# Distance between the two operands' addresses in products of 256 columns

## The chip, the cores and the metric

One core of a Trainium2 chip runs the whole kernel. The metric is device time in microseconds of one execution; the time of a kernel is the median of its runs.

## The reference

One block of an encoder for a sequence of 1024 tokens with 1024 channels, all in float32. The input is normalised and multiplied by one wide matrix, which feeds three mixers side by side: dilated sliding-window attention, grouped-query attention with normalised and rotated queries and keys, and cross-attention to 256 memory rows. Each has a gate, is projected, and the three are merged, projected once more, normalised and added to the input. Cut to what bears on this change:

```python
h = rms_norm(x, g_pre[layer])
a_qkv, bq, bk, bv, mq, ga, gb, gm, mg = jnp.split(h @ w_in[layer], split_at, axis=-1)
...
qb_ = axial_rope(rms_norm(bq.reshape(b, s, B_HEADS, HEAD_DIM), q_norm[layer]), row_pos, col_pos)
kb_ = axial_rope(rms_norm(bk.reshape(b, s, B_KV_HEADS, HEAD_DIM), k_norm[layer]), row_pos, col_pos)
...
kvm = rms_norm(mem, g_mem[layer]) @ w_mem_kv[layer]
km, vm = ...   # 4 heads of 128, 256 memory rows
sm = jnp.einsum('bshd,bnhd->bhsn', mq.reshape(b, s, M_HEADS, M_HEAD_DIM), km)
pm = jax.nn.softmax(sm * (M_HEAD_DIM ** -0.5), axis=-1)
om = jnp.einsum('bhsn,bnhd->bshd', pm, vm)
```

## The kernel before, in words

Every float32 matrix is split into a high part, rounded to the type that TensorE multiplies in one pass, and a low part, the rest. A product of two matrices is then three products: high by high, low by high, high by low. `hh[k]` and `hl[k]` (k = 0 to 7) are the high and low part of the normalised input, 128 channels by 1024 tokens each; `wh` and `wl` those of a tile of weights.

A product has two operands in on-chip memory: the one that is loaded into the array first (128 columns here; the profile calls it LDWEIGHTS) and the moving one, which is streamed through it (256 or 512 columns). In this text "weights" is the loaded operand, whatever it holds. In `PE.matmul(dst, a, b)` the weights are `a`, the moving operand is `b`.

The first stages, in the order in which they run:

1. `kv_proj` (line 354): keys and values of the grouped-query attention for all tokens. Eight tiles of channels, eight of tokens, three products each: 192 products, weights `hh` or `hl`, moving `wbh` or `wbl` with 256 columns. The operands of tile k are made by ScalarE (`hh`, line 255) and VectorE (`hl`, line 256) while the products of the tile before run. Behind the first half of its last tile stand eight transposes (line 242).
2. Two gate units (lines 128, 130, 132): products of 512 columns, beside which the norms of the keys run on VectorE, ScalarE and GpSimd.
3. `add_kv` (line 526): keys and values of the memory, eight units of 24 products; weights `wh` or `wl`, moving `mh` or `ml`, 256 columns.
4. Query units, woven together: `proj_tok` (lines 284, 286, 288) has 384 products, weights `hh` or `hl`, moving `wbh` or `wbl`, 256 columns. `m_att`, the memory attention, uses `passes` (line 110) for its scores (weights `mqh`, `mql`, moving `kmh`, `kml`) and its values (weights `vmh`, `vml`, moving `mph`, `mpl`), 192 products of 256 columns. Between them stand units of 512 columns (lines 128 to 132) and transposes (lines 590 and 700).

```python
for k in range(8):                                                   # proj_tok
    PE.matmul(dst, hh[k][:, t], th[:, k], start=k == 0, stop=False)
    PE.matmul(dst, hl[k][:, t], th[:, k], start=False, stop=False)
    PE.matmul(dst, hh[k][:, t], tl[:, k], start=False, stop=k == 7)
...
passes(sv[:, j], [(qh[:, t], kmh[:, h]), (qh[:, t], kml[:, h]), (ql[:, t], kmh[:, h])])   # scores
terms += [(vmh[:, kt, h], ph[:, kt]), (vmh[:, kt, h], pl[:, kt]), (vml[:, kt, h], ph[:, kt])]
passes(o[:, 0:256], terms)                                           # values
```

The order on TensorE is written out by the program (`weave` takes turns between two generators by costs in nanoseconds that are written in the code); addresses play no part in it. Behind these stages come the grouped-query attention (lines 775 to 809), the value projection (line 1314, products of 512 columns alone) and the rest.

Tiles come from pools, which hand out addresses in the order of the calls. The pool `st` (input tiles `xk`, later `mh` and `ml` in their places, tables) and, when it has closed, `qn` and `mt` (tiles of the memory attention) grow from the left; `kvl`, `ml` and `mb` (`wbh`, `wbl`, tables of the queries) lie at the right end, each placed against its right neighbour, so that a longer `mb` begins further left. A pad is a tile that nothing uses: it only moves what stands behind it (or, in a pool at the right, what stands ahead of it). A tile of weights of 128 columns is 512 bytes long in each partition, and all slices of 128 columns of one tile have one address modulo 512. In the kernel before, the address of the moving operand and that of the weights are equal modulo 512 in every product of 256 or 512 columns but the 128 of line 809 (the attention's values, 64 columns of weights) and the 6 of line 1977.

Of the kernel before, what the change touches and what calls it, by code (L numbers as in the profile page):

```python
# [8 lines left out]
F32 = mybir.dt.float32  # L9
# [8 lines left out]
P = 128  # L18
# [15 lines left out]
def block(ctx: ExitStack, tc: tile.TileContext, x, xT, memT, cst, msk, bcst, tabA, gpost,  # L34
# [28 lines left out]
    def pss1():  # L63
        return bank["p"].tile([P, 512], F32, name="s1", tag="s1", bufs=bank["n"][1])

    def pst():
        bank["i"] += 1
        return bank["p"].tile([P, 4, 128], F32, name="tr", tag="t", bufs=bank["n"][2])

    def pso():  # L70
        return bank["p"].tile([P, 512], F32, name="ov", tag="o", bufs=bank["n"][3])
# [17 lines left out]
    def split(dst_h, dst_l, src):  # L89
        A.activation(dst_h, src, AF.Copy)  # L90
        V.tensor_tensor(dst_l, src, dst_h.bitcast(F32), op=OP.subtract)  # L91
# [15 lines left out]
    def passes(out_ps, terms):  # L107
        n = len(terms)
        for i, (a, b) in enumerate(terms):
            PE.matmul(out_ps, a, b, start=i == 0, stop=i == n - 1)  # L110
# [107 lines left out]
    def pool(name, side="left"):  # L218
        p = tc.tile_pool(name=name, bufs=1, side=side, reuse_waits="tile")
        return p, p.__enter__()  # L220
# [4 lines left out]
    startp, st = pool("start")  # L225
    kvp, kvl = pool("kvl", "right")
    mlp, ml = pool("ml", "right")
    mbp, mb = pool("mb", "right")
# [4 lines left out]
    vmh = ml.tile([P, 2, 4, 128], R, name="vmh")  # L233
    vml = ml.tile([P, 2, 4, 128], R, name="vml")

    xk = [st.tile([P, S], F32, name=f"xk{k}") for k in range(8)]
    acc = st.tile([P, S], F32, name="acc")

# [27 lines left out]
    def fetch_wb(c0):  # L266
        raws = []
        for i in range(2):
            raw = wp.tile([P, 1024], F32, name="wr", bufs=WR)
            raws.append(raw.rearrange("p (k f) -> p k f", k=4))  # L270
        return raws, mb.tile([P, 8, 256], R, name="wbh"), mb.tile([P, 8, 256], R, name="wbl")
# [162 lines left out]

    PROJ = 8 * 24 * 109.0
    raws, *wkv = fetch_wb(512)
    mb.tile([P, 112], F32, name="pad")

    def load_wkv(i):
        nc.sync.dma_start(raws[i // 2][:, i % 2 * 2:i % 2 * 2 + 2], wb[:, 2 * i:2 * i + 2, 512:768])  # L440
# [113 lines left out]
    QN = [ql_.tile([P, 8, 64], F32, name=f"qn{T}") for T in range(NT)]  # L554
    mtp, mt_ = pool("mt")
    fp["p"] = mt_

    def m_att(h):
        qh, ql = MQ[h]
        if h == 0:  # L560
            mt_.tile([P, 48], F32, name="pad")
        for _ in range(4):
            yield 250
        st = {}

        def scores(n):
            sv = pss1().rearrange("p (t k) -> p t k", t=2)
            nm = mt_.tile([P, 2], F32, name="mnm", bufs=3)
            l = mt_.tile([P, 2], F32, name="mls", bufs=3)
            pm = mt_.tile([P, 2, 256], F32, name="pm", bufs=2)  # L570
            for j in range(2):
                t = slice((2 * n + j) * 128, (2 * n + j) * 128 + 128)
                passes(sv[:, j], [(qh[:, t], kmh[:, h]), (qh[:, t], kml[:, h]), (ql[:, t], kmh[:, h])])
            V.tensor_reduce(nm, sv, axis=AX.X, op=OP.min)
            V.tensor_tensor(nm, nm, rcol[:, 2 * n:2 * n + 2], op=OP.mult)
            for j in range(2):
                A.activation(pm[:, j], sv[:, j], AF.Exp, scale=nrcol[:, 2 * n + j:2 * n + j + 1], bias=nm[:, j:j + 1],
                             accum_out=l[:, j:j + 1])
            rl = mt_.tile([P, 2], F32, name="mrl", bufs=4)
            V.reciprocal(rl, l)  # L580
            for j in range(2):
                fp["mv"] = V.tensor_scalar(pm[:, j], pm[:, j], rl[:, j:j + 1], None, op0=OP.mult)
            st[n] = pm

        def trans(n):
            pm = st[n]
            tp = pst().rearrange("p (k t) q -> p k t q", k=2)
            for kt in range(2):
                for j in range(2):
                    PE.transpose(tp[:, kt, j, :], pm[:, j, kt * 128:kt * 128 + 128], ident)  # L590
            ph = mt_.tile([P, 2, 256], R, name="mph", bufs=2)
            pl = mt_.tile([P, 2, 256], R, name="mpl", bufs=2)
            split(ph, pl, tp.rearrange("p k t q -> p k (t q)"))
            st[n] = (ph, pl)

        def pv(n):
            ph, pl = st.pop(n)
            o = pso()
            terms = []
            for kt in range(2):  # L600
                terms += [(vmh[:, kt, h], ph[:, kt]), (vmh[:, kt, h], pl[:, kt]), (vml[:, kt, h], ph[:, kt])]
            passes(o[:, 0:256], terms)
            om = mt_.tile([P, 256], F32, name="om", bufs=2)
            A.activation(om, o[:, 0:256], AF.Copy)
            nc.sync.dma_start(od[2, h, :, n * 256:n * 256 + 256], om)

        for n in range(7):
            if n < 4:
                scores(n)
            yield 654  # L610
            if 0 <= n - 2 < 4:
                trans(n - 2)
            yield 436
            if 0 <= n - 3 < 4:
                pv(n - 3)
            yield 654
# [46 lines left out]
    early[len(queue)] = lambda: load_w(wu[U_G + 11])  # L663
    weave(1)
    weave(2, m_att(0), M_COST, 1.2)
    weave(2, m_att(1), M_COST, 1.2)
    weave(1, m_att(2), M_COST, 1.0)
    weave(1, m_att(3), M_COST, 1.0)
    while pend:
# [1692 lines left out]
```

## Time and profile before

| what | value |
|---|---|
| median of 3 runs | 1372.11 us (1370.52 to 1373.05) |
| the profiled execution's own time | 1370.94 us |
| its span, first to last instruction | 1369.1 us |
| TensorE clock granted, mean | 0.998 |
| TensorE busy | 1349.7 us, 99% of the span |
| VectorE, ScalarE, GpSimd busy | 74%, 48%, 42% |
| products on TensorE | 8303 records |

The durations that the profile gives for a product hold its way through the array and overlap with those of its neighbours (a product of 256 columns is shown as some 283 ns). How long a product takes in a stream is the distance from one start to the next; it is read from the chain of work, where rows of equal products are merged with their count, or from the starts in the timeline.

### The profile page before, as it was taken

The page shows a single profiled execution, that of the slowest core. Times are in us where ns is not written, and L with a number is a line of the kernel's source. Part 1 is how long each engine was busy: PE and PEld are TensorE (multiplying, and loading weights), DVE is VectorE, ACT ScalarE, POOL GpSimd, SP SyncE. Part 2 cuts the span into 40 slices and gives each one's busy share as a digit, 9 for nine tenths or more (in the row PEclk, how much of TensorE's full clock was granted, in tenths as well). Part 3 has the DMA queues.
Part 4 walks back from the last instruction along what each step waited for, and adds up shares of the span by engine and source line. Part 5 has one row for each costly group of instructions (what it writes and reads, how often), then busy time and mean ns, then how long its engine had stood idle before and what let it go on. Part 6 is the DMA issues. An engine that isn't in the chain of part 4 may idle for free.

```text
span 1369.1 us, 22888 instructions
## 1 busy us (share of the span) xinstructions
PE 1349.7 (99%) x8303; PEld 1091.0 (80%) x8303; DVE 1018.1 (74%) x1836; ACT 655.5 (48%) x1388; POOL 579.8 (42%) x443
## 2 busy tenths in 40 slices
PE   8999999999999999999999999999999999999997
PEld 7899987666666788988888888888888777778886
DVE  7868667777777398767777786687877666768977
ACT  7544456656654445333333333333335676763332
POOL 0516702666577200244465554555552134663003
PEclk9999999999999999999999999999999999999999
DMA  6356522222244569524333333322347778986455
GB/s 252 108 170 215 186 109 101 100 74 98 74 126 147 203 219 286 163 70 127 112 108 124 108 123 116 114 94 92 110 127 256 234 213 239 271 233 227 148 189 185
DMA packets 125489, 213.81 MB, mean 156 GB/s; under 512 B 32480, under 2 KB 64576, under 8 KB 125376
## 3 DMA queue, kind: packets, MB, share of 16 engines
q1 hardware_dynamic: 116064, 198.42, 45.2%
q10 hardware_dynamic: 9312, 13.93, 2.8%
q8 instruction: 65, 1.06, 0.3%
q14 instruction: 48, 0.39, 0.1%
HBM read 145.92 MB, written 66.38 MB: 155 GB/s over the span
## 4 chain that ended last, share of the span: by engine, by line
PE 92%; DVE 2%; POOL 2%; ACT 1%; issue 1%; DMA 1%; SPq 0%; DVEq 0%; POOLq 0%; ACTq 0%
PE s L1314 35%; PE d L1903 6%; PE s L1224 4%; PE s L2127 4%; PE ov L809 3%; PE sc L2045 3%; PE d L130 3%; PE d L128 3%; PE d L132 3%; PE s L1275 3%; PE s L1587 2%; PE tr L775 2%; PE s L794 2%; PE s L793 2%; PE d L526 2%; PE d L2127 2%
## 5 line engine op out<-in xcount | busy, mean ns | idle before, releaser
L800 POOL TENSOR_TENSOR bl<-bl,bp 128x512 f32<-128x512 f32 x96 | 133.0, 1385 | 54.1 <-ACT bp L796 48.6
L1314 PE MATMUL s<-hh,vS 128*128 128x512 f32 x400 | 131.1, 389 | 0.0
L1314 PE MATMUL s<-vA,vS 128*128 128x512 f32 x450 | 106.1, 389 | 0.0
L91 DVE TENSOR_TENSOR vS<-vot,vS 128x512 fp32r<-128x512 f32 x75 | 89.4, 1192 | 19.9 <-ACT vS L90 19.9
L1314 PEld LDWEIGHTS s<-vA,vS 128*128 128x128 f32 x450 | 84.5, 188 | 17.5
L796 ACT ACTIVATE bp<-s 128x512 f32<-128x512 f32 x128 | 75.6, 595 | 43.9 <-PE s L794 42.9
L776 DVE TENSOR_REDUCE bn<-tr 128x1 f32<-128x512 f32 x128 | 85.0, 684 | 13.7 <-PE tr L775 12.6
L132 PE MATMUL d<-hh,wl 128*128 128x512 f32 x224 | 89.4, 399 | 0.0
L128 PE MATMUL d<-hh,wh 128*128 128x512 f32 x224 | 89.2, 398 | 0.0
L130 PE MATMUL d<-hl,wh 128*128 128x512 f32 x224 | 89.1, 398 | 0.0
L1314 PEld LDWEIGHTS s<-hh,vS 128*128 128x128 f32 x400 | 75.1, 188 | 15.6
L1599 ACT ACTIVATE pra<-pra,sts 128x192 f32<-128x192 f32 (+1 forms) x176 | 72.4, 415 | 12.5 <-DVE sts L1598 12.1
L1314 PE MATMUL s<-hh,wl 128*128 128x512 f32 x200 | 78.1, 391 | 0.0
L1314 PE MATMUL s<-hl,wh 128*128 128x512 f32 x200 | 77.9, 389 | 0.0
L1314 PE MATMUL s<-hh,wh 128*128 128x512 f32 x200 | 77.8, 389 | 0.0
L1314 PE MATMUL s<-hl,vS 128*128 128x512 f32 x200 | 77.8, 389 | 0.0
L1598 DVE CUSTOM_DVE_ANT_0 pra<-s,mask 128x192 f32<-128x192 f32 (+1 forms) x192 | 48.9, 309 | 33.3 <-PE s L1587 18.7
L1058 POOL TENSOR_TENSOR vot<-wr 128x512 f32<-128x512 f32 x13 | 22.2, 1706 | 111.4 <-DVE wl L91 111.4
L1318 ACT ACTIVATE vv<-s 128x512 f32<-128x512 f32 x50 | 29.9, 598 | 82.4 <-PE s L1314 48.5
L809 PE MATMUL ov<-bp,VS 128*64 128x512 f32 x256 | 58.5, 598 | 0.0
L1058 POOL TENSOR_TENSOR vot<-vot,vA 128x512 f32<-128x512 f32 x12 | 19.3, 1606 | 89.7 <-DVE vS L91 89.7
L128 PEld LDWEIGHTS d<-hh,wh 128*128 128x128 f32 x224 | 42.2, 188 | 13.4 <-issue 5.5
(626 smaller groups left out, 4012.3 us busy)
## 6 DMA issues: line engine op xcount, KB each, us to landing
wr<-in_wu SPq DMA_DIRECT2D x40, 512.0 KB
vA<-in_wu SPq DMA_DIRECT2D x24, 512.0 KB
qkd<-ko SPq DMA_DIRECT2D x96, 128.0 KB
wl<-thd SPq DMA_DIRECT2D x24, 512.0 KB
wos<-os SPq DMA_DIRECT2D x12, 512.0 KB
wr<-in_wbr SPq DMA_DIRECT2D x24, 256.0 KB
aq<-qkd SPq DMA_DIRECT2D x12, 512.0 KB
ak<-qkd SPq DMA_DIRECT2D x12, 512.0 KB
```

Source lines behind the costliest of these rows:

```text
L91: V.tensor_tensor(dst_l, src, dst_h.bitcast(F32), op=OP.subtract)
L128: PE.matmul(dst, wh[:, k, :], hh[k][:, t], start=k == 0, stop=False)
L130: PE.matmul(dst, wh[:, k, :], hl[k][:, t], start=False, stop=False)
L132: PE.matmul(dst, wl[:, k, :], hh[k][:, t], start=False, stop=k == 7)
L776: fp["last"] = V.tensor_reduce(st[i]["n"][:, j, c:c + 1], s, axis=AX.X, op=OP.min)
L796: A.activation(pp, s, AF.Exp, scale=-1.0)
L800: G.tensor_tensor(lsum[i % 2], lsum[i % 2], pp, op=OP.add)
L809: PE.matmul(o[e * 64:e * 64 + 64], VS[:, kt, kv], d.pop(kt), start=kt < 2, stop=kt >= NT - 2)
L1314: PE.matmul(BANK[n, c], a, b, start=k == 0 and q == 0 and not more, stop=k == 3 and q == 2, skip_group_check=c in "XW")
L1599: A.activation(src, src, AF.Exp, scale=-1.0, bias=bias, accum_out=sts[:, 1, h, T:T + 1])
L1903: PE.matmul(ps_, a, b, start=k == 0 and q == 0, stop=k == 3 and q == 2)
L2127: PE.matmul(dst[:, e[0]:e[1]], a, b, start=k == 0 and q == 0, stop=k == 3 and q == 2)
```

## The change

Three pads are changed. A pad of 112 elements (448 bytes, which is 64 short of 512) is taken out of `mb` and one of the same size put at the start of `st`. In `mt`, a pad of 48 elements (192 bytes) becomes one of 16 (64 bytes), and another of 16 is put at the pool's start.

```diff
+    st.tile([P, 112], F32, name="pad")
     xk = [st.tile([P, S], F32, name=f"xk{k}") for k in range(8)]
...
     raws, *wkv = fetch_wb(512)
-    mb.tile([P, 112], F32, name="pad")
...
     mtp, mt_ = pool("mt")
     fp["p"] = mt_
+    mt_.tile([P, 16], F32, name="pad")
 
     def m_att(h):
         qh, ql = MQ[h]
         if h == 0:
-            mt_.tile([P, 48], F32, name="pad")
+            mt_.tile([P, 16], F32, name="pad2")
```

The addresses in bytes that come of it, with what is left modulo 512:

| operand | before | after |
|---|---|---|
| `hh0`, weights of lines 354, 284, 288 | 22496 (480) | 22496 (480) |
| `wbh`, moving there | 175584 (480) | 176032 (416) |
| `mh0`, moving in line 526 (its weights lie at 480) | 120800 (480) | 121248 (416) |
| `mqh`, weights of the memory scores | 137184 (480) | 137248 (32) |
| `kmh`, moving there | 200672 (480) | 200672 (480) |
| `vmh`, weights of the memory values | 208864 (480) | 208864 (480) |
| `mph`, moving there | 158176 (480) | 158112 (416) |

So in all 960 products of 256 columns of these lines the moving operand now starts at the weights' address less 64, modulo 512. The products of 256 columns of two later lines (1275 with 336, 2127 with 24) and all those of 512 columns keep equal addresses.

On every engine the same instructions stand in the same order as before, with the same operands. Three waits fall away, since the tiles of `mt` now lie a little beside tiles that had the place before: that of the first reduction over memory scores and of the first exponential (line 577) on GpSimd, and that of the first load of the output weights on TensorE. The line numbers of the changed kernel are higher by one between the first pad and the second, and again behind the third.

## The prediction

> **What bounds the kernel now.** I read the page first, then who waited for whom on TensorE, then the chain of work piece by piece through the first 228 us, then single products in the timeline.
>
> ```profile
> PE 1349.7 (99%) x8303; PEld 1091.0 (80%) x8303; DVE 1018.1 (74%) x1836; ACT 655.5 (48%) x1388; POOL 579.8 (42%) x443
> PE 92%; DVE 2%; POOL 2%; ACT 1%; issue 1%; DMA 1%; SPq 0%; DVEq 0%; POOLq 0%; ACTq 0%
> ```
>
> The first line is busy time by engine, the second the shares of the chain that ended last. TensorE is on that chain for 92% of the span, so a shorter or longer product is a shorter or longer kernel unless something else then arrives late. The waits of TensorE, next, say how much else is late now.
>
> ```profile
> PE s L354 <- ACT hh L255: 6.6, 1, 6.6
> PE s L1941 <- DVE acc L1377: 0.9, 1, 0.9
> PE d L526 <- DVE fth L201: 0.6, 1, 0.6
> PE tr L775 <- DVE bn L776: 0.6, 1, 0.6
> ```
>
> Columns: total us, times, longest. The 6.6 us are the start, before the first operand exists. In the stages of the change there is one wait of 0.6 us (L526) and one of 0.6 us right behind them (L775). TensorE runs without a pause otherwise, and the start-to-start distance of its products, which I call the pace, is what sets the time.
>
> The pace of the products of 256 columns stands in the chain (start us, us, what, count):
>
> ```profile
> 7.40 4.00 PE s L354 x17
> 11.40 0.91 PE ov L354 x6
> 12.31 2.16 PE s L354 x18
> 14.46 0.72 PE ov L354 x6
> ...
> 31.02 0.87 PE tr L242 x8
> ...
> 65.73 2.88 PE d L526 x24
> ...
> 95.39 0.72 PE s L110 x6
> ...
> 639.99 80.12 PE s L1314 x353
> ```
>
> 2.16 us for 18, 0.72 for 6, 2.88 for 24: 120.0 ns each, in three different stages, to the last digit. The first 23 products (17 and 6) take 4.91 us, 213 ns each: that is the start of the kernel, which the change does not touch. The last row is the pace of 512 columns in a long undisturbed stage: 80.12 / 353 = 227.0 ns. From 256 to 512 columns the pace grows by 107.0 ns, so 256 columns by themselves cost 107.0 and each product carries 120.0 - 107.0 = 13.0 ns on top, at either width. Those 13 ns are all that this change can work on. The eight transposes of L242 have 128 moving columns and 128 columns of weights and take 0.87 / 8 = 108.8 ns each; moving alone would be half of 107, so it is the weights' load that takes the 108.8. I take this as the least pace that a product with 128 columns of weights can have.
>
> The Trainium skill, "TensorE: Matmul & The Clock Gate", section "Back-to-back issue gap", gives N / 2.4 + 2.5 ns for an isolated product at full clock, an estimate of 109.2 ns for 256 columns; by it 10.8 ns of the 120.0 would be to be had, 10.1 us in all. The trace's 120.0 is far from it, so something else takes time here.
>
> **The change part by part.** No instruction is added, removed or reordered on any engine. Three pads move, and with them the tiles behind them, so that in every product of 256 columns of the first stages the moving operand starts 64 bytes below a multiple of 512 from the weights, where before the two are equal modulo 512. The groups by shape give the number of products (48 x 3 + 16 x 3 in L354; 64 x 6 in L284, L286 and L288; 64 x 3 in L526; 32 x 6 in L110), one row of each line here:
>
> ```profile
> L526 PE MATMUL d<-mh,wh 128*128 128x256 f32 x64 | 18.9, 295 | 0.6 <-DVE fth L201 0.6
> L286 PE MATMUL s<-wbh,hl 128*128 128x256 f32 x64 | 18.3, 285 | 0.0
> L354 PE MATMUL s<-wbh,hh 128*128 128x256 f32 x48 | 14.6, 305 | 6.6 <-ACT hh L255 6.6
> L354 PE MATMUL ov<-wbh,hl 128*128 128x256 f32 x16 | 4.7, 291 | 0.0
> L110 PE MATMUL ov<-mph,vmh 128*128 128x256 f32 x32 | 9.1, 285 | 0.0
> ```
>
> 192 + 384 + 192 + 192 = 960, of which 23 belong to the start: 937 products at 120 ns. One ns on the pace is 0.94 us of the kernel. About 0.2% (2.7 us) is what a measurement of this kernel can tell from no change, so the change shows from 2.9 ns on.
>
> What does the distance between two addresses do to a pace? The trace has no stage with another distance, but it shows that the pace is not one number. While a product runs, the weights of the next are loaded, both from the same memory:
>
> ```profile
> L284 PEld LDWEIGHTS d<-wbh,hh 128*128 128x128 f32 x64 | 12.3, 192 | 0.0
> L128 PEld LDWEIGHTS d<-hh,wh 128*128 128x128 f32 x125 | 23.5, 188 | 4.3
> ```
>
> Beside products of 256 columns the same load of 128x128 takes 192 ns, beside those of 512 columns 188. And after a product of another kind the two streams meet differently for a while:
>
> ```profile
> 199.93 0.28 PE L110 MATMUL s<-kmh,mqh 128*128 128x256 f32 x1
> 200.04 0.27 PE L110 MATMUL s<-kml,mqh 128*128 128x256 f32 x1
> 200.16 0.28 PE L110 MATMUL s<-kmh,mql 128*128 128x256 f32 x1
> 200.27 0.28 PE L110 MATMUL s<-kmh,mqh 128*128 128x256 f32 x1
> 200.39 0.28 PE L110 MATMUL s<-kml,mqh 128*128 128x256 f32 x1
> 200.51 0.28 PE L110 MATMUL s<-kmh,mql 128*128 128x256 f32 x1
> 200.63 0.39 PE L132 MATMUL d<-hh,wl 128*128 128x512 f32 x1
> ```
>
> Six products in 200.63 - 199.93 = 0.70 us, 116.7 ns each, the first two 115. So 120.0 is a rhythm into which long runs fall, not the least that this kernel reaches at 256 columns; in that rhythm the load is longest. I read it as load and moving operand getting in each other's way, and 64 bytes between their addresses as another meeting of the two. The price of the new pace lies between the weights' load alone, 108.8 (gain 11.2 x 0.937 = 10.5 us), and a loss that I bound by products of 512 columns that are out of their rhythm:
>
> ```profile
> 212.76 0.40 PE L130 MATMUL d<-hl,wh 128*128 128x512 f32 x1
> 212.99 0.40 PE L132 MATMUL d<-hh,wl 128*128 128x512 f32 x1
> 213.23 0.40 PE L128 MATMUL d<-hh,wh 128*128 128x512 f32 x1
> 213.47 0.60 PE L700 MATMUL tr<-cs,qn 128*128 128x128 f32 x4
> ```
>
> Three in 0.71 us, 236.7 each, 9.7 ns above 227.0 (loss 9.1 us). My value is 113, the middle between 108.8 and the 116.7 of the six products: 7.0 ns less, 937 x 7.0 = 6.6 us. I lean to the gain because at this width the rhythm is the slow one of the two states that the trace shows, and a shift of addresses is what could break it.
>
> Does the gain reach the end? The other engines have room in these stages (busy us of each in windows of the projection of keys, memory keys, query projections, last query units):
>
> ```profile
> 12.00:34.00 22.00, 22.00 (x183) 21.86 (x182) 21.26 (x28) 17.53 (x25) 1.04 (x2) 1.00 0.63 239
> 56.00:82.00 26.00, 25.41 (x212) 25.03 (x211) 21.05 (x35) 16.25 (x29) 3.56 (x4) 1.00 0.50 163
> 93.00:168.00 75.00, 75.00 (x572) 72.38 (x571) 56.89 (x140) 32.86 (x79) 52.07 (x77) 1.00 0.54 189
> ```
>
> The columns behind the length are PE, PEld, DVE, ACT, POOL, then clock, DMA share and GB/s. VectorE is busy 81% of the second window and 76% of the third; a pace 6% shorter leaves it below 87%. Only the first is tight, 97%: there VectorE makes the operands that the products eat. Its last ones are these:
>
> ```profile
> 25.99 1.41 DVE L256 SCALAR_TENSOR_TENSOR hl<-xk,cs,hh 128x512 fp32r<-128x512 f32 x2
> ```
>
> They end at 27.4. The products that read them are the last 24 of the stage, and the eight transposes stand in their middle: twelve run ahead of 31.02, so they begin at 31.02 - 12 x 0.12 = 29.6. From 12.3 to 29.6 a pace of 113 wins 17.3 x 7 / 120 = 1.0 us: they start at 28.6, still 1.2 us behind their operand. So I take the whole gain as passed on; the two waits of 0.6 us could grow by the 1.0 us of the first stage at the worst.
>
> Beside that, small: the identity transposes of these stages get a new distance too (64 bytes more), but they run at 108.8, the load's own pace, and there are 92 of them; I cost them at nothing (2 ns either way would be 0.2 us). The products of 512 columns keep their addresses. Three waits on tiles that no longer share a place fall away (a reduction and an exponential of the first memory scores, and the first load of the output weights); TensorE waits for none of them, so nothing. The sum: 1370.9 us, the profiled execution's own time, less 6.6. That execution lies 1.2 us under the median of the runs, 1372.1; carried to the median the sum is **1365.5 us**.
>
> **The rivals.** *Equal addresses are the good place.* The pads of before put all these operands at equal addresses modulo 512, the rhythm of 227.0 at 512 columns is the shortest there (236.7 out of it), and a fixed distance of 64 bytes may make every product meet the load in its middle. Then the pace goes up instead: between nothing and 9.7 ns, and I take 6 ns, 937 x 6 = 5.6 us, 1377.7. It decides from 122.9 ns on. Against it: at 256 columns the state out of rhythm was shorter, not longer.
>
> *Out of rhythm, no new one.* The products wander, as the six above, between 116.7 and 120; at 118.5 that is 937 x 1.5 = 1.4 us, 1370.7, within what can't be told apart.
>
> *The addresses do not matter.* Then the 13 ns belong to every product whatever it reads, and the time stays 1372.1. What speaks for it is that the 13 ns are the same at 256 and 512 columns; against it, that the load takes 188 or 192 and the pace 116.7 or 120 with the same shapes. The Trainium skill, "SBUF — State Buffer", section "Who interferes with whom", is on its side: TensorE has two read ports, one for the moving operand and one for the weights' load, independent of each other. By that rule no distance would change anything; the two load times above do not fit it well.
>
> **How the numbers follow.** A new, shorter rhythm 0.46; wandering 0.12; no effect 0.10; a longer pace 0.32. Faster by over 0.2% is the first, 0.46; within 0.2% the next two, 0.22; slower the last, 0.32. The range goes from the load's own pace, 1372.1 - 10.5 = 1361.6, to 6.3 ns above the pace of now, 1372.1 + 5.9 = 1378.0; beyond its upper end lies a part of the last case, about 0.12, and below it about 0.05. The likeliest case by itself: 1361.6 to 1369.4.
>
> **What would show it.** Right: in the chain after, 24 products of L526 take about 2.71 us instead of 2.88 and six of L110 0.68 instead of 0.72; the load in L284 falls under 192; TensorE's waits stay as they are; L1314 stays at 80.12 for 353. Wrong: 2.88 again (no effect), or 3.0 and more (the first rival); or a shorter pace with longer waits at L526, L354 or L775, which would mean that the gain was taken back by VectorE.

## The result and the profile after

The kernel before took 1372.17 us (median of 9 runs, 1370.52 to 1373.46), the changed one 1369.01 us (9 runs, 1366.62 to 1369.09): ratio 0.9972, 95% interval 0.9963 to 0.998. That is 3.2 us less, where 6.6 were forecast. A second set of runs on the same kernels gave 1371.01 and 1367.70 us, ratio 0.9976 (0.9966 to 0.9986). The profiled execution after has an own time of 1369.01 us and a span of 1367.2; the chip granted the same clock, 0.998.

Line numbers in the other kernels differ from those of the kernel before, by one less to five more; L354 of before is L355 after, L284 is L285, L1314 is L1315.

The pace first. The timeline of TensorE after shows two units of L526 (start us, us, then engine, line, operation, names). The four rows are the second and the last product of one unit, and the second and the last of another one:

```profile
70.26 0.28 PE L526 MATMUL d<-ml,wh 128*128 128x256 f32 x1
72.77 0.28 PE L526 MATMUL d<-mh,wl 128*128 128x256 f32 x1
...
76.27 0.28 PE L526 MATMUL d<-ml,wh 128*128 128x256 f32 x1
78.86 0.28 PE L526 MATMUL d<-mh,wl 128*128 128x256 f32 x1
```

There are 22 steps in each pair: 2.51 us, 114.1 ns a product, in the first unit; 2.59 us, 117.7 ns, in the second. Same line, same tiles, same distance of 64 bytes: this distance has two rhythms. The exact spacings are 113, 113, 114 over and over (mean 113.3) in the one, once its first steps (120, 116, 116) are over, 118, 118, 117 (mean 117.7) in the other. Before, most spacings were 120 (141 of 174 in L526).

Over whole stages, start to start from each product to the next instruction, in ns, without gaps of 150 ns and more (means from all records of the trace):

| stage | before | after | products |
|---|---|---|---|
| L354 / L355 | 120.05 | 113.6 | 170 |
| L526 | 119.7 | 115.3 | 183 |
| L284 to L288 / L285 to L289 | 119.75 | 115.1 | 375 |
| L110 | 119.2 | 115.9 | 190 |

The sum of the gains is 170 x 6.4 + 183 x 4.4 + 375 x 4.6 + 190 x 3.3 ns = 4.2 us. The weights' load beside these products, from the instructions of line L526, before and after (min, median and max in ns, then first and last start):

```profile
L526 PEld LDWEIGHTS d<-mh,wh x64: 186/192/192, 56.9 to 81.3; 128*128 128x128 f32 x64
```

```profile
L526 PEld LDWEIGHTS d<-mh,wh x64: 187/188/193, 55.9 to 79.4; 128*128 128x128 f32 x64
```

192 has become 188, the duration that the load has beside products of 512 columns. Those products have kept their pace, as the chain after shows for the undisturbed stage (397 in 90.16 us, 227.1 each):

```profile
639.86 90.16 PE s L1315 x397
```

Then the waits of TensorE after (total us, times, longest):

```profile
PE s L355 <- ACT hh L256: 6.3, 1, 6.3
PE tr L1654 <- DMA avs<-vdr: 1.4, 2, 0.9
...
PE d L526 <- DVE fth L201: 0.6, 1, 0.6
...
PE tr L776 <- DVE bn L777: 0.5, 1, 0.5
PE d L132 <- DVE wl L91: 0.4, 1, 0.4
...
PE s L110 <- ACT pm L578: 0.3, 1, 0.3
PE tr L243 <- DVE acc L264: 0.3, 1, 0.3
```

The waits at L526 and for `bn` at L776 stand as before. New in these stages are those at L243, L132 and L110, all three in or right behind the stages that became quicker. The chain after shows who released the first two:

```profile
26.58 0.74 DVE hl L257
27.33 1.15 DVE acc L264
28.57 1.24 DVE acc L264
29.85 1.09 PE tr L243 x8
...
72.70 1.14 DVE wl L502
73.86 4.63 DMA wr<-in_wu
78.60 1.07 ACT wh L90
79.69 1.24 DVE wl L91
80.97 0.50 PE d L132
```

Before, the chain ran through TensorE here (L354 x18, then the transposes). Now, at 29.85, the transposes start when VectorE has added up the squares (`acc`), and at 80.97 the first product with low weights starts when a transfer, ScalarE and VectorE have made them. VectorE has nothing left in the first stage (busy us of PE, PEld, DVE, ACT, POOL in the window):

```profile
12.00:34.00 22.00, 21.71 (x183) 21.22 (x183) 21.75 (x30) 17.35 (x25) 1.70 (x2) 1.00 0.65 242
```

21.75 of 22.00 us, 99%. Told from the first product of TensorE, the same product comes earlier than before by (two profiled executions of the changed kernel):

| up to | first profile | second profile |
|---|---|---|
| end of the first stage | 0.65 us | 0.53 us |
| before L526 | 0.71 | 0.59 |
| behind L526 | 1.52 | 1.40 |
| first query unit | 0.82 | 1.05 |
| end of the memory attention | 2.87 | 3.27 |
| last product | 1.59 | 1.55 |

In the first profile the wait for `acc` widens the spacing at the first transpose to 562 ns, against 122 before: 0.44 us. At L132 two spacings of 831 and 338 ns stand for two of some 235: 0.70 us. At the first product of L110 behind `pm` one of 615 stands for 117: 0.50 us. Together 1.6 us, and 4.2 less 1.6 is 2.6, close to the 2.87 found.

A small part of the table is not the change. At the start of the kernel products are 206 ns and more apart; this held for 20 spacings in the profile before, 19 in the first and 18 in the second after, which is 0.10 and 0.18 us of every row.

What the last row of the first profile lost on top, 1.3 us, differs between executions of the same kernel: a quarter of a microsecond each at 289 us (`QL` at L776) and 529 us (`hl` at L1225), the rest over a millisecond into the kernel, in part at transfers (`avs` at L1654: 0.6 us in the profile before, 1.4 here). The second profile gained 0.3 us at L1225 and lost 2.0 over the last 300 us.

### The profile page after: what moved, and what is told of

It is laid out like the page before. It is cut to its first block, busy times and chain, and to the rows that moved or that the text cites. A ratio compares the mean times of both kernels' runs of the same rounds, so it can differ in the third digit from the quotient of the medians.

```text
span 1367.2 us, 22887 instructions
## 1 busy us (share of the span) xinstructions
PE 1346.3 (98%) x8303; PEld 1087.8 (80%) x8303; DVE 1016.8 (74%) x1836; ACT 655.3 (48%) x1388; POOL 579.4 (42%) x443
## 4 chain that ended last, share of the span: by engine, by line
PE 81%; DVE 6%; DMA 5%; ACT 3%; issue 2%; POOL 2%; SPq 1%; DVEq 0%; ACTq 0%; POOLq 0%
PE s L1315 35%; PE d L1904 6%; PE s L2128 4%; PE ov L810 3%; PE sc L2046 3%; PE s L1276 3%; PE d L132 3%; PE d L130 3%; PE d L128 3%; PE s L1588 2%; PE tr L776 2%; PE s L794 2%; PE s L795 2%; DMA vrt<-rld 2%; PE d L2128 2%
## 5 line engine op out<-in xcount | busy, mean ns | idle before, releaser
L1315 PE MATMUL s<-hh,vS 128*128 128x512 f32 x400 | 131.3, 390 | 0.0
L1315 PE MATMUL s<-vA,vS 128*128 128x512 f32 x450 | 106.1, 390 | 0.0
L1315 PEld LDWEIGHTS s<-vA,vS 128*128 128x128 f32 x450 | 84.5, 188 | 17.5
L132 PE MATMUL d<-hh,wl 128*128 128x512 f32 x224 | 89.8, 401 | 0.4 <-DVE wl L91 0.4
L1315 PEld LDWEIGHTS s<-hh,vS 128*128 128x128 f32 x400 | 75.2, 188 | 15.5
L1315 PE MATMUL s<-hh,wl 128*128 128x512 f32 x200 | 78.2, 391 | 0.0
L1315 PE MATMUL s<-hl,wh 128*128 128x512 f32 x200 | 78.0, 390 | 0.0
L1315 PE MATMUL s<-hh,wh 128*128 128x512 f32 x200 | 78.0, 390 | 0.0
L1315 PE MATMUL s<-hl,vS 128*128 128x512 f32 x200 | 77.9, 390 | 0.0
```

The lines of the kernel that those rows point to most:

```text
L132: PE.matmul(dst, wl[:, k, :], hh[k][:, t], start=False, stop=k == 7)
L1315: PE.matmul(BANK[n, c], a, b, start=k == 0 and q == 0 and not more, stop=k == 3 and q == 2, skip_group_check=c in "XW")
```

## The experiments

All are made from the kernel before or after by pads alone, unless said otherwise. "Distance" is the address of the moving operand less that of the weights, modulo 512. Most kernels here ran once; as eight runs of the changed kernel spread from 1365.24 to 1369.53 us, a single time says little, and these kernels are read by the paces in their traces.

**What does a distance do?** Three kernels from the one before, each with two distances, `wbh`/`wbl` for L285 to L289 and L355, `mh`/`ml` for L527:

```diff
-    mb.tile([P, 112], F32, name="pad")
+    mb.tile([P, 96], F32, name="pad")     # 448 - 4*96 = +64;  120: -32;  16: -128
...
+    st.tile([P, 120], F32, name="pad")    # 4*120 - 512 = -32;  64: 256;   8: +32
     xk = [st.tile([P, S], F32, name=f"xk{k}") for k in range(8)]
```

> The kernel before with two other pads: the moving operand 64 bytes behind the weights modulo 512 (+64) in the key and query projections (L355, L285 to L289), 32 in front (-32) in the memory keys (L527), equal in the memory attention (L111). Theory (the pace of a product follows from its own distance, and equal addresses are a slow place): L111 stays at 120 in long runs; the two others leave 120.0, and which way is open, between 113 and 128. Rival 1 (any distance but zero is as good as -64): L355 and L285 to L289 at 113 to 118, L527 the same. Rival 2 (the sign decides, the moving operand has to be in front): +64 at 122 or more, -32 at 113 to 118. Whole time: 1367 to 1370 by rival 1, up to 1378 by rival 2.

> The kernel before with -32 in the key and query projections (L355, L285 to L289) and half of 512 (256) in the memory keys (L527). Theory (each distance has its own pace): two different paces, neither 120.0. Rival 1 (any distance but zero): both 113 to 118. Rival 2 (in front, by less than a part of 512): -32 at 113 to 118, 256 as at zero or worse.

> The kernel before with -128 in the key and query projections and +32 in the memory keys (L527). Theory: two paces of their own. Rival 1: both 113 to 118. Rival 2 (sign): -128 at 113 to 118, +32 above 120.

Measured: 1368.77, 1369.08 and 1370.37 us in one run each, the kernel before 1371.47 on the same chip. The chain shows the pace of L355, 18 products in a row, first at +64, then at -32, then at -128:

```profile
14.95 2.12 PE s L355 x18
```

```profile
15.12 2.13 PE s L355 x18
```

```profile
15.04 2.14 PE s L355 x18
```

117.8, 118.3 and 118.9 ns; at equal addresses it was 2.16. At +32, L527 of the third kernel has 24 in

```profile
68.25 2.81 PE d L527 x24
```

that is 117.1 ns. At 256 bytes the pace is that of equal addresses, 119.6, and so is the load, 192 ns. So neither "any distance other than zero will do" nor "the sign decides" holds: 256 acts as 0, and distances on both sides of 0 are quicker.

**The missing distances, and does the line matter?** The same two pads again:

```diff
-    mb.tile([P, 112], F32, name="pad")
+    mb.tile([P, 8], F32, name="pad")      # -96;  104: +32
...
+    st.tile([P, 16], F32, name="pad")     # +64;   24: +96
```

> The kernel before with the wide K and V weights at -96 bytes from the moving operand (L285 to L289, L355) and the start's mh at +64 (L527); the scores and the values of the memory attention stay at equal addresses. Theory (every distance has a pace of its own, whatever the tile): +64 gave 117.8 in L285 to L289, so L527 shows 117.5 to 118.2; -96 lies between -64 (115.1) and -128 (118.6), so 116 to 118 in L285 to L289. Rival (the pace belongs to the place of the line, not to the distance): L527 at +64 shows 115 to 116, as it does at -64. Sum by the theory: 375 products by 2.7 ns and 183 by 1.8 ns, 1.3 us, less some 0.5 of new waits: 1371.3 of 1372.1.

> The kernel before with the wide K and V weights at +32 bytes from the moving operand (L285 to L289, L355) and the start's mh at +96 (L527); the rest at equal addresses. Theory (every distance has a pace of its own, whatever the tile): +32 gave 116.9 in L527, so L285 to L289 show 116.5 to 117.3; +96 lies between +64 (117.8) and 256 (119.6), 117 to 119 in L527. Rival (the pace belongs to the place of the line): L285 to L289 at +32 show 117.8 as they do at +64. Sum by the theory: 375 products by 2.9 ns and 183 by 1.5, 1.4 us, less some 0.5 of new waits: 1371.2 of 1372.1.

Measured: 1369.6 and 1370.13 us in one run each (before 1370.87), 1.3 and 0.7 us less. The paces, with those of the other kernels:

| distance | mean pace, ns, and where |
|---|---|
| 0 | 119.5 to 120.1, short rows of L110 118.7 to 119.2 |
| 256 | 119.6 (L527) |
| -32 | 118.4 (L527), 118.0 to 118.6 (L285 to L289, L355) |
| -64 | rhythms of 113.3 and 117.7, all lines; whole stages from 113.5 to 117.8 |
| -96 | 117.3 to 118.1 (L285 to L289, L355) |
| -128 | 118.4 to 118.9 (L285 to L289, L355) |
| +32 | 116.9 (L527), 116.7 to 117.5 (L285 to L289, L355) |
| +64 | 117.6 to 118.0 (L285 to L289, L355), 116.7 (L527), 114.8 and 117.3 (L1276, in kernels below) |
| +96 | 119.9 (L527), single spacings from 113 to 125 |

+64 in L527 gave 116.7 instead of the expected 117.5 to 118.2: about a quarter of its spacings were 113 or 114, so +64 has the quick rhythm as well. Its mean runs from 114.8 to 118.0 with the line: a distance alone does not fix the mean, since it depends on how much of a row falls into which rhythm. The ranges of +32, +64, -32, -96 and -128 overlap, and whether each has a pace of its own is not shown. +96 missed its range by 0.9 ns at the upper end. Its load took 188 ns, as at -64, beside the slow pace of 0, so the load's duration does not tell the pace. No distance that was tried gave a whole stage a lower mean than -64 did (113.5).

**Is it the distance or the place of the moving operand, and do 512 columns want it too?** One pad of 64 bytes ahead of the weights' tiles moves `wh` and `wl` and the pools behind them, and nothing of `hh`:

```diff
+    wp.tile([P, 16], F32, name="padw", bufs=1)
     extra = []
```

> The kernel before with one pad of 64 bytes ahead of the tiles wh and wl and all pools behind them: hh and hl stay. The gate units (L129 to L133), the products L1315 with wh and wl, L1904 and L2046 (512 columns) have their moving operand at -64, L1225 (512) and L1276 (256 columns) at +64, the products of vA by vS in L1315 stay equal. Theory (distance, not place): the 512 columns at -64 leave 226.7 though their moving operand has not moved; if the 13 ns of 120.0 and 227.0 are one thing, they go to 220 (6.7 less, as 256 columns went from 120.0 to 113.3) and the kernel gets 10 us or more shorter. Rival (place of the moving operand): L129 to L133 stay at 226.7, L1276 changes. Rival (256 columns alone, since there the load takes as long as the product): 512 columns go up, to the 231 to 237 seen out of rhythm, 10 to 20 us longer.

Measured: 1379.36 us in one run, 7.9 us above the kernel before. `hh` and `hl` stand where they stood. In L1276 the 288 products of 256 columns whose moving weights now lie at +64 went from 120.0 to 114.8. The other 48, and all of L527, have both operands moved by 64 and so kept distance 0: they stayed at 119.8 and 119.7. L285 to L289 and L355, where nothing moved, stayed at 119.5 to 119.9. So the distance acts, not the place of a tile. At 512 columns it acts the other way: products at -64 take 233.1 to 233.5 ns (L1315, L1904, L2046, at equal addresses 226.8, 230.8 and 226.9), at +64 229.0 to 230.3. The products of L1315 that are still at equal addresses take 228.8 on the mean: behind a displaced row up to ten spacings scatter between 224 and 236, then the row is back at 226 and 227. The chain shows the stage as a whole, 230.3 a product instead of 227.1:

```profile
639.82 90.27 PE s L1315 x392
```

The guess of 220 for 512 columns was wrong, by sign; of the two rivals the one that kept the gain to 256 columns was right in direction, though the kernel lost 7.9 us and not the 10 to 20 that it named.

**What gives the gain back: the first stage.** The last Square and the last add into `acc` are issued in halves, so that the first four transposes need only the first half:

```diff
-            A.activation(xk[k], xk[k], AF.Square)
-            V.tensor_tensor(acc, acc, xk[k], op=OP.add)
+            for t in ([slice(0, 512), slice(512, 1024)] if k == 7 else [slice(0, S)]):
+                A.activation(xk[k][:, t], xk[k][:, t], AF.Square)
+                V.tensor_tensor(acc[:, t], acc[:, t], xk[k][:, t], op=OP.add)
```

> The changed kernel, with the Square and the add into acc of the last x tile issued in two halves of 512 elements, so that the first four transposes of acc need only the first half. Theory (part of the quicker pace is given back by new waits, one of them of the first transposes of L243 on the sum in acc, where the product before is 562 ns ahead of the next instead of some 113): that wait falls from 0.3 us to under 0.1, everything behind it on TensorE lies some 0.4 us earlier, the pace of the products stays at 113 to 116 ns, and the time is 1368.5, between 1368.0 and 1369.0. Rival (the wait stands in for one that comes later, so that removing it gives nothing): the row of waits is gone, the first product of L527 begins no more than 0.1 us earlier, time 1369.0. Rival (two small instructions cost VectorE and ScalarE more than one long one and the row sums are later): the wait grows to 0.5 us, time 1369.3.

Measured: 1368.46 us in one run (before 1370.87). The wait is gone, but this run can't decide between the theories, since the stage ran in the slow rhythm from the start to its end. The chain, 18 products in 2.12 us, 117.8 each:

```profile
15.56 2.12 PE s L356 x18
17.68 0.71 PE ov L356 x6
18.39 2.12 PE s L356 x18
20.51 0.71 PE ov L356 x6
```

The products were too slow to be early for `acc`, the start took 23 spacings instead of 20, which is 0.3 us, and the stage ended 0.05 us ahead of before. It shows something else: the same distance in the same line runs in either rhythm, here for some 160 products on end. The stage was in the quick one in four profiles with -64 (113.5 to 113.6) and in the slow one in three (117.6 to 117.75); the products' order and distance in it were the same in all seven profiles.

**What gives the gain back: the late weights.** The changed kernel with `mh` and `ml` at equal addresses again:

```diff
-    st.tile([P, 112], F32, name="pad")
     xk = [st.tile([P, S], F32, name=f"xk{k}") for k in range(8)]
```

> The changed kernel with one part undone: the pad ahead of the x tiles is left out, so that the 192 products of L525 have their operands at equal addresses modulo 512 again, and all others stay at 64 bytes in front. Plain sum: their pace goes back from 115.3 to 119.7 ns, 183 of them by 4.4 ns make 0.8 us, and the time is 1369.8. Theory (this part of the gain was given back at once, since the first product with the low weights of the gate and query stage waits 0.43 us for VectorE's wl and the products around it lose some 0.7 us): with products that arrive 0.8 us later that wait is gone (under 0.1 us), the first query unit begins no more than 0.2 us later than in the changed kernel, time 1369.1. Rival (the wait follows the transfers, which move with TensorE): the wait stays at 0.4 us and the time is 1369.8.

Measured: 1368.45 us in one run, 2.4 us under the kernel before on its chip, where the changed kernel was 3.2 and 3.3 under; one run can't tell these apart. L525 is back at 119.65 ns. The wait at L132 is not among its waits any more, as expected, but the first query unit began 0.95 us later than in the changed kernel and not 0.2 at the most: 0.76 of that arose ahead of L525, where the products are the same in both. Between the start of L525 and the first query unit the changed kernel of the first profile gained 0.11 us on the one before, this one lost 0.09: of the 0.8 us that the quicker L526 won, 0.2 were left. In other executions of quick L526 more was left: 0.46 in the second profile of the changed kernel, 0.83 in the kernel below that has `wh` of L1276 at -64, and 0.87 in the kernel with halves above, where nothing was given back. So what is given back at L132 differs by execution; in the first profile it was the transfer that set it.

The first stage shows its bound in this run too. TensorE waits 0.7 us for `acc`, and the spacing at the first transpose is 970 ns. The chain:

```profile
27.93 1.15 DVE acc L263
29.16 1.24 DVE acc L263
30.45 1.09 PE tr L242 x8
```

`acc` came 0.6 us later than in the first profile of the changed kernel, and the transposes with it, 0.6 us later. They start when `acc` is there, and how quick the products were no longer matters.

**The changed kernel again, and the same step for a later stage.** The first kernel is the changed one as it is. The other two give the high weights of L1276, the other stage with products of 256 columns, a distance of their own: buffers of `wh` 512 bytes wider, and a view that starts 448 bytes (that is -64) or 64 bytes into them.

```diff
+    def whtile(c=0, dt=R):
+        return wp.tile([P, 1152], dt, name="wh")[:, c:c + 1024]
...
-        h, l = wslot(0), wslot(1)
+        h, l = wslot(0, 112), wslot(1)      # 112: -64;  16: +64
```

> The changed kernel as it is, beside the next two on the same chip: 1369.0 us, 3 us under the kernel before (2.4 to 3.6). Theory (which of the two rhythms a stretch of products runs in follows from the order and the start of the products, not from chance): the paces of its stages are those of the first profile to 0.3 ns: L355 113.6, L526 115.3, L285 to L289 114.9 to 115.3, L110 115.9. Rival (the rhythm falls anew in each execution): they differ by 1 ns or more in at least one stage.

> The changed kernel, with the same step taken for the later stage that has products of 256 columns: the buffers of the high weights wh are 512 bytes wider, and the moving high weights of L1276 (224 of its 336 products) lie 64 bytes in front of the weights' addresses modulo 512; the low ones (112) stay at equal addresses for want of room, and all products of 512 columns stay at equal addresses. Theory (distance -64 gives 113.3 or 117.7 ns, whatever the line, and the dense stretch passes its gain on): the 224 products go from 120.0 to between 113.5 and 117.7, the low ones stay between 118 and 120, together 0.5 to 1.6 us less, time 1368.0, between 1367.4 and 1368.6. Rival (the distance to the next product's weights decides as much as a product's own, so that a mixed row loses the gain): 119 or more on the mean, time 1369.0. Rival (a wait behind the stage takes the gain): the pace falls, the first product of L1315 comes 1 us earlier, and the time stays at 1369.0.

> As the kernel with the high weights of L1276 at -64, with these at +64 instead. Theory: +64 gave 114.8 in this line when all of its weights lay there, 116.7 in L527 and 117.8 in L285 to L289; the 224 products come to between 114.5 and 118, together 0.4 to 1.2 us less, time 1368.2, between 1367.6 and 1368.8. Rival (the distance to the next product's weights decides as much): 119 or more on the mean, time 1369.0.

Measured, five rounds on one chip, the kernel before 1371.01 us there:

| kernel | median, us | ratio to before | interval |
|---|---|---|---|
| changed, again | 1367.70 | 0.9976 | 0.9966 to 0.9986 |
| with `wh` of L1276 at -64 | 1366.94 | 0.9969 | 0.9958 to 0.9981 |
| with `wh` of L1276 at +64 | 1366.70 | 0.9967 | 0.9956 to 0.9979 |

The changed kernel repeats its paces: 113.5, 115.3, 115.1 and 115.9. In the second kernel the high products of L1276 go from 120.0 to 116.65 and the low ones stay at 119.96, 0.74 us in all; the median is 0.76 lower. In the third it is 117.26 and 122.14, 0.37 us in all. Both medians lie below the expected ranges (1367.4 to 1368.6 and 1367.6 to 1368.8), which were reckoned from 1369.0 for the changed kernel; told from its 1367.70 here, 0.76 and 1.00 less are within the 0.5 to 1.6 and 0.4 to 1.2 expected. But the 0.37 us of the third kernel's trace is short of that and explains a third of its 1.00, and the intervals overlap: that both beat the kernel before is shown, that they beat the changed one is not.

The paces of these two kernels in their first stages speak against order alone choosing the rhythm: L358 ran at 117.75 in the second kernel and at 113.6 in the third. Both had come early to full pace (13 spacings of 206 ns and more at the start, 19 and 18 in the two profiles of the changed kernel), and the number of these spacings does not sort the rhythms: 13, 18, 19 and 22 in the quick profiles, 13, 23 and 23 in the slow ones. The third kernel's timeline at the end of the first stage, TensorE and then VectorE:

```profile
28.61 0.28 PE L358 MATMUL s<-wbl,hh 128*128 128x256 f32 x1
30.02 1.09 PE L246 MATMUL tr<-cs,acc 128*128 128x128 f32 x8 [1.14 <-DVE acc L267]
```

```profile
27.42 2.55 DVE L267 TENSOR_TENSOR acc<-acc,xk 128x1024 f32<-128x1024 f32 x2
```

A product starts at 28.61, the transposes at 30.02: 1.41 us apart, all but 0.1 of it waiting for the two adds that end at 29.97. The products had won 1.27 us by the 100th, 0.77 of it from the shorter start; at the end of the stage 0.47 was left. The second kernel, in the slow rhythm, was early for `acc` as well, by 0.40 us: its start alone had won 0.67.

**Both together**: the high weights of L1276 at -64, and `acc` in halves.

> The kernel with the high weights of L1276 at -64 as well, and with the Square and the add into acc of the last x tile in two halves of 512. Theory (at the first transposes TensorE waits for the sum in acc; the halves let the first four begin 0.6 us earlier): with the quick rhythm in the first stage (113.3) the spacing at the first transpose, 517 to 1411 ns in the runs of the changed address, falls to under 500, and the end of the stage lies 0.9 to 1.1 us ahead of the kernel before instead of 0.5 to 0.65; with the slow rhythm (117.7) there is no wait to remove and the end lies 0.1 to 0.6 ahead. Time 1366.6, between 1365.9 and 1367.4. Rival (the two halves, 1.37 us instead of 1.22, make the last four transposes late by as much): the wait only moves to the fifth transpose, the end of the stage lies 0.5 to 0.65 ahead as without halves, time 1366.9.

Measured: 1367.01 us, before 1370.85, ratio 0.9965 (0.9952 to 0.9977); as quick as without the halves, within the intervals. In the profiled execution the first stage took the slow rhythm again (117.7), did not wait for `acc`, and ended 0.10 us ahead of before. That the halves would help in the quick rhythm was not shown: in both kernels with them the stage ran in the slow one. Whether that is chance or comes from the halves stays open.

## Why the forecast was right in direction and too large

*What bounds it.* Right: TensorE's pace set the time of these stages, and a shorter pace made the kernel shorter.

*A shift of 64 bytes breaks the slow rhythm.* Right, and it was the point that could have gone either way. Equal addresses are the slow place at 256 columns: eight distances were tried, and only 256 and +96 are as slow as 0. The load in L526 fell from 192 to 188 ns as expected of L284, but as +96 shows, a load of 188 goes with the slow pace too, so it is no proof of the mechanism that the forecast read into it; how operands at equal addresses slow a product stays open. The rival of no effect falls. The Trainium skill, "SBUF — State Buffer", section "Who interferes with whom", gives TensorE two independent read ports, one for the moving operand and one for LDWEIGHTS. By that alone no distance would matter; here 64 bytes between the two addresses, with nothing else changed in a product, are worth 2 to 7 ns of pace.

*The rival that equal addresses are the good place.* Wrong at 256 columns, and right at 512, where 64 bytes cost 6.7 ns in L1315. The forecast took its bound for a loss from products of 512 columns (9.7 ns); that was a fair size for them and the wrong shape for this change. So the 13 ns that the forecast put on top of both widths are not one term: the shift that takes from them at 256 columns adds to them at 512.

*The size of the term: 113 ns.* This step failed by its size. 113 was the middle between the load's 108.8 and the 116.7 of six products. That the quick rhythm is 113.3 is luck, since nothing in that middle points to a rhythm; and a third of the products run in the other, 117.7, so that the mean is 115.0. Also, the pace before was 119.7 on the mean of the four stages, not 120.0: some 4.6 ns of gain instead of 7.0, 4.2 us instead of 6.6. The short rows of six in L110, which begin behind products of 512 columns, are mostly in the slow rhythm; the estimate of 0.68 us for six was that of the quick one.

*The whole gain is passed on.* This step failed too. The forecast looked for the operand that the last products need (`hl`, ready at 27.4), found 1.2 us of room, and did not ask what the transposes behind the first twelve of them need. They need `acc`, which VectorE finishes behind the last `hl` in its queue. The profile before had both times, VectorE's last adds and TensorE's first transpose:

```profile
27.32 2.55 DVE L263 TENSOR_TENSOR acc<-acc,xk 128x1024 f32<-128x1024 f32 x2
30.86 0.82 PE L242 MATMUL tr<-cs,acc 128*128 128x128 f32 x6
```

`acc` was ready at 29.87, so the room was 1.0 us, no more than the gain forecast for this stage. (The second row has six of the eight transposes.) It became a wait because the room differs by execution: over the 14 profiles `acc` was ready 22.9 to 24.4 us behind the first product, 23.25 in the profile before and 23.50 in the first one after, where the first product began 0.32 us earlier in the span and `acc` was ready at about the same time. Told from the span's start, the transposes of that profile came 1.0 us earlier, at 29.85. All four executions in the quick rhythm reached the transposes 0.4 to 1.3 us too early. The other wait, for the low weights at the first gate unit behind L526, was not seen at all. It took 0.70 us of the 0.8 in the first profile, 0.35 in the second, and between nothing and 0.56 in four other executions. The text had named a shorter pace with longer waits as what would mean that VectorE takes the gain back; it came at L243, L132 and L110, not at L526, L354 or L775.

*The rest.* The transposes kept their pace (109 ns), as costed at nothing. Products of 512 columns kept theirs.

So 6.6 became 4.2 by the rhythm, and 1.3 to 1.6 us less by the new waits, which leaves 2.6 and 2.9; 2.9 and 3.3 were found at the end of the memory attention, 0.10 and 0.18 of it from the start. The medians of the two sets of runs were 3.2 and 3.3 us lower, but the two profiled executions were only 1.6 ahead at their last product: for the whole kernel the account closes to about a microsecond.

What stays open is why a stretch of products takes the one rhythm or the other. In the first stage it differed between kernels whose products are the same, while the two profiles of the changed kernel agree. In the woven query units it changes at nearly the same products in the four profiles with a quick first stage (364 of the 384 are alike). In the other three, those with a slow first stage, 38 more products between 140 and 147 us are slow, and the mean is 115.6 instead of 115.1. So the choice is not made by the order alone, and the two stages, over 100 us apart, go together in all seven; what links them no run shows.

## What to carry to other kernels

Where rows of equal products run without a pause, compare their start-to-start time with that of other rows of the same shape, and look at the addresses of the two operands: here 64 bytes were worth up to 6.7 ns on 120, in opposite directions for 256 and 512 columns, so each width has to be measured by itself. When an engine becomes quicker, take for every instruction behind the quick stretch, not only for the products in it, the time at which its operands are ready, and read from the other engine's timeline how early it may come. The room that one profile shows, behind a transfer or behind another engine, differs between executions by as much as such a gain, and so does the start of the kernel.

## What had not been expected of the hardware

- One distance has two stable rhythms (113.3 and 117.7 ns at -64), each kept for some 160 products on end. Which one a stretch of the query units took went with the rhythm of a stage 100 us earlier, in seven profiles of seven.
- At 256 bytes, the one other multiple tried, pace (119.6) and load (192 ns) are those of 0.
- At 512 columns the best distance tried is 0 (226.7 ns), and behind a displaced row it can take ten products at 0 (224 to 236 ns) before that rhythm is back.
- No distance reached the 109.2 ns that the Trainium skill, "TensorE: Matmul & The Clock Gate", section "Back-to-back issue gap", gives by its formula for an isolated product of 256 columns, an estimate; the least spacing kept over a row was 113.3.
